# Hybrid decoder block: own-block mask applied once per head on GpSimd, score sums negated

## The chip, the core and the metric

The kernel runs on one NeuronCore of one Trainium2 chip. The metric is device time in microseconds (us) of one execution; lower is better. Engines are named as in the profile: PE (TensorE matmul), PEld (TensorE weight load), DVE (VectorE), ACT (ScalarE), POOL (GpSimd) and SP (SyncE, which only issues DMAs). Each engine works through its own instruction queue in order.

## The reference, cut to the attention branch

One decoder layer, 512 tokens, width 1024. A gated DeltaNet branch (8 heads) and a forgetting-attention branch (8 heads of 128) run on one input projection, are merged by sigmoid gates, and a squared-ReLU MLP of width 4096 follows. The change touches the forgetting attention alone:

```python
def forgetting_attention(q, k, v, log_f):
    cum = jnp.cumsum(log_f, axis=-1)
    scale = FOX_DH ** -0.5
    for i in range(t // FOX_BLOCK):          # 4 blocks of 128 queries
        q0, q1 = i * FOX_BLOCK, (i + 1) * FOX_BLOCK
        s = (jnp.einsum('bhqd,bhkd->bhqk', q[:, :, q0:q1], k[:, :, :q1]) * scale
             + cum[:, :, q0:q1, None] - cum[:, :, None, :q1])
        mask = (q0 + jnp.arange(FOX_BLOCK))[:, None] >= jnp.arange(q1)[None, :]
        p = jax.nn.softmax(jnp.where(mask, s, -jnp.inf), axis=-1)
        outs.append(jnp.einsum('bhqk,bhkd->bhqd', p, v[:, :, :q1]))
```

## The kernel before, in words

Weights stream through the core once. Each unit of weights (128x1024 float32) is loaded into a raw tile, rounded by ACT into `hi` (L243, in the MLP L1366) and subtracted by DVE into `lo` (L244, L1373), so that PE can multiply in three passes. In the second half of the input projection (`stream`, L988, tiles `st`) and in the MLP the weights are combined in a Strassen-like scheme: some raw tiles are first loaded by SP (L204) and later changed in place by an accumulating DMA that POOL issues (L208, `sraw`).

The branches run as generators (`fox_worker`, `head`, `group_chain`, `decays`, ...) that `tick()` advances between pieces of the projection. What comes out is a program order; a scheduler of the framework then fixes the order on each engine's queue from its own estimate of when inputs are ready. A change of one instruction can therefore move others.

`fox_worker` handles one attention head at a time (two workers from the middle of the kernel on). For a head it takes `nr`, a 128x512 tile `row` in which every partition holds the negated forget sums of the head's 512 keys; SP loads it (L530, `row<-rowd`, one of three `row` buffers). Then: squares of q and k (ACT L859, DVE L860, L861), a power on POOL (L335, `fss`), scaling of q and k on POOL (L865), transposes on PE, copies to `qT`, `kT` on ACT (L878, L879). Then for each of the four query blocks i, with n = 128(i+1) keys:

- the bias tile (two buffers): ACT adds the query's own sum to the first n-128 columns (L892, not for i = 0), and DVE writes the last 128 columns as row + sum + causal mask (L893, `scalar_tensor_tensor`, from the SBUF tiles `nr` and `caus`);
- PE multiplies q and k (L896, `sc`), DVE adds the bias and takes the row maximum in one instruction (L899, shown as CUSTOM_DVE), DVE negates the maximum (L901, a 128x1 `tensor_scalar`), ACT takes the exponential with that shift and sums it (L902);
- one step later DVE inverts the sum and scales (L908, L909), PE transposes (L912, `pT`), ACT copies out (L914), and a step later PE multiplies by v (L921, `fo`).

At the same time the second DeltaNet group runs: `head` (L588, L590, L606, L630, L639, L641 on POOL) and `invert` (L655 to L687, `X`, `tmp`).

Of the kernel before, what the change touches and what calls it, by code (L numbers as in the profile page):

```python
# [6 lines left out]
                             make_lower_triangular, make_upper_triangular)  # L7

F32 = mybir.dt.float32
F32R = mybir.dt.float32r  # L10
AF = mybir.ActivationFunctionType
ALU = mybir.AluOpType
# [4 lines left out]
P = 128  # L17
# [4 lines left out]
NCH = T // P  # L22
# [22 lines left out]
def hybrid_block(tc, a, out):  # L45
    nc = tc.nc
# [20 lines left out]
    def nm(s):  # L67
        n_names[0] += 1
        return f"{s}_{n_names[0]}"
# [5 lines left out]
    def page(dt=F32, s="pg"):  # L75
        if s in FOX_TAGS:
            return fxp.tile([P, T], dt, tag=s, name=nm(s))
        tag = TAGS_OF.get(s, s)
        if tag in TAGS:
            return pgp.tile([P, T], dt, tag=tag, name=nm(s), bufs=TAGS[tag])  # L80
        return pgp.tile([P, T], dt, tag="pg", name=nm(s))
# [3 lines left out]
    def const(shape, s, dt=F32):  # L85
        return (cp if s in KEEP else cm).tile(shape, dt, tag=s, name=s)

    def small(n, s="sm"):
        return smp.tile([P, n], F32, tag="sm", name=nm(s))
# [12 lines left out]
    def atps(s="at"):  # L102
        return pat.tile([P, T], F32, tag="at", name=nm(s))

    def v3(ap, n):
        return ap.rearrange("p (a b) -> p a b", a=n)

    def bc(ap, n):
        return ap.unsqueeze(2).to_broadcast(list(ap.shape) + [n])

    def cs(c):
        return slice(c * P, (c + 1) * P)

    mm = nc.tensor.matmul
    vec, act, pool = nc.vector, nc.scalar, nc.gpsimd
# [23 lines left out]
    def start(gen):  # L139
        tasks.append(gen)  # L140
        return gen
# [3 lines left out]
    def store_late(dst, src):  # L145

        for _ in range(LATE):
            yield
        nc.sync.dma_start(dst, src)
# [169 lines left out]

    upper = const([P, P], "upper")  # L320
    make_upper_triangular(nc, upper, diag=True)
    caus = const([P, P], "caus")
    make_causal_mask(nc, caus, mask_val=-1e30)
    slow_ = const([P, P], "slow_")
    make_lower_triangular(nc, slow_, diag=False)
    slow = const([P, P], "slow", F32R)
# [7 lines left out]
    def rsq(dst, src):  # L334
        pool.tensor_tensor(dst, src, expo[:, 0:src.shape[-1]], op=ALU.pow)  # L335
# [115 lines left out]
    cc = const([P, NCH, H], "cc")  # L451
# [387 lines left out]
    def bias_rows(n):  # L839

        if n < len(fq) and n not in rows_of:
            rows_of[n] = row_page(2, fq[n][0])
        return rows_of.get(n)

    def fox_worker(after=None):

        while after is not None and not inverted[after]:
            yield
        while taken[0] < H:
            if taken[0] >= len(fq) or hold[0]:  # L850
                yield
                continue
            h, qk, vt = fq[taken[0]]
            nr = bias_rows(taken[0])
            taken[0] += 1
            sq = small(16, "fss")
            for half in range(2):
                junk = page(s="junk")
                act.activation(junk, qk[half], AF.Square)  # L859
                vec.tensor_reduce(sq[:, 4 * half:4 * half + 4], v3(junk[:, :], 4), axis=AX.X, op=ALU.add)  # L860
            vec.tensor_scalar(sq[:, 0:8], sq[:, 0:8], 1.0 / P, EPS, op0=ALU.mult, op1=ALU.add)  # L861
            rsq(sq[:, 8:16], sq[:, 0:8])
            for half in range(2):
                t = v3(qk[half][:, :], 4)
                pool.tensor_tensor(t, t, bc(sq[:, 8 + 4 * half:12 + 4 * half], P), op=ALU.mult)  # L865
            yield
            yield
            bias_rows(taken[0])
            ptq = atps("fqT")
            ptk = atps("fkT")  # L870
            for tb in range(NCH):
                t = qk[tb // 2]
                i = tb % 2
                nc.tensor.transpose(ptq[:, cs(tb)], t[:, cs(2 * i)], ident)
                nc.tensor.transpose(ptk[:, cs(tb)], t[:, cs(2 * i + 1)], ident)
            qT = page(s="fq")
            kT = page(s="fk")
            act.activation(qT, ptq, AF.Copy, scale=fqs)  # L878
            act.activation(kT, ptk, AF.Copy, scale=fk_g)  # L879
            yield  # L880
            while not vt:
                yield
            po = None
            st = {}
            for step in range(NCH + 2):
                i = step
                if i < NCH:
                    n = (i + 1) * P
                    s = cs(i)
                    bias = page(s="bias")  # L890
                    if i:
                        act.activation(bias[:, :n - P], nr[:, :n - P], AF.Identity, bias=cc[:, i, h:h + 1])  # L892
                    vec.scalar_tensor_tensor(bias[:, s], nr[:, s], cc[:, i, h:h + 1], caus,  # L893
                                             op0=ALU.add, op1=ALU.add)
                    psc = atps("sc")
                    mm(psc[:, :n], qT[:, s], kT[:, :n], start=True, stop=True)  # L896
                    sm = small(4, "fsm")
                    pt = page(s="p")
                    vec.tensor_tensor_reduce(out=pt[:, :n], in0=psc[:, :n], in1=bias[:, :n], scale=1.0,  # L899
                                             scalar=-3.0e38, op0=ALU.add, op1=ALU.max, accum_out=sm[:, 0:1])  # L900
                    vec.tensor_scalar(sm[:, 1:2], sm[:, 0:1], -1.0, None, op0=ALU.mult)  # L901
                    act.activation(pt[:, :n], pt[:, :n], AF.Exp, bias=sm[:, 1:2], accum_out=sm[:, 2:3])  # L902
                    st[i] = [pt, sm]
                i = step - 1
                if 0 <= i < NCH:
                    n = (i + 1) * P
                    pt, sm = st[i]
                    vec.reciprocal(sm[:, 3:4], sm[:, 2:3])  # L908
                    vec.tensor_scalar(pt[:, :n], pt[:, :n], sm[:, 3:4], None, op0=ALU.mult)  # L909
                    pT = atps("pT")  # L910
                    for c in range(i + 1):
                        nc.tensor.transpose(pT[:, cs(c)], pt[:, cs(c)], ident)  # L912
                    pTs = page(s="pTs")
                    act.copy(pTs[:, :n], pT[:, :n])  # L914
                    st[i] = pTs
                i = step - 2
                if 0 <= i < NCH:
                    if po is None:
                        po = atps("fo")
                    for c in range(i + 1):  # L920
                        mm(po[:, cs(i)], vt[c], st[i][:, cs(c)], start=(c == 0), stop=(c == i))  # L921
                yield
            o = page(s="ob")
            act.copy(o, po)
            stores.append(start(store_late(obd[h], o)))
# [139 lines left out]
    box = {}  # L1065
    start(decays(0, box, gt))
    fws = [start(fox_worker())]
    ch0 = gdn_group(0, box)
    fox_pair(0)
# [7 lines left out]
    hold[0] = False  # L1077
    finish(fu)
    fws += [start(fox_worker()) for _ in range(1, NFW)]


# [272 lines left out]
    for k, (w, c, p, s_) in enumerate(MLP):  # L1354
# [6 lines left out]
        n = pos[0]  # L1361
# [121 lines left out]
```

## Time and profile before

| | before |
|---|---|
| median of 3 runs | 999.35 us (997.99 to 1000.86) |
| profiled execution | 998.66 us, of which the span is 997.0 us |
| PE busy | 979.5 us (98%) |
| DVE busy | 721.9 us (72%) |
| ACT busy | 595.7 us (60%) |
| POOL busy | 233.1 us (23%) |
| granted TensorE clock | 1.00 over the span |

The span runs from the first to the last instruction; 1.66 us of the profiled execution lie around it. An idle time stands in square brackets behind an instruction, with what ended it: `[0.56 <-DVE p L909]` means that the engine stood idle for 0.56 us until L909 was done. An engine that shows no bracket was busy until then.

### The profile page before, as it was taken

The numbers are of one execution on the slowest core, as the hardware profiler recorded it, in microseconds if no ns is written. First come the engines' busy times: TensorE is split into PE (matmuls) and PEld (weight loads), VectorE is DVE, ScalarE is ACT, GpSimd is POOL, SyncE is SP. The second block draws the span as 40 slices with busy tenths as digits, with TensorE's granted clock in tenths as the row PEclk, the third lists the DMA queues.
The fourth block names the chain that finished last, engine by engine and source line by source line (L and its number), as shares of the span: only waits on it lengthen the run. The fifth ranks groups of instructions, "written<-read, shape, count | busy, mean of one in ns | idle before, by whom it ended". The sixth has DMA issues, their size and how long they took to land.

```text
span 997.0 us, 17216 instructions
## 1 busy us (share of the span) xinstructions
PE 979.5 (98%) x6545; PEld 880.3 (88%) x6545; DVE 721.9 (72%) x1268; ACT 595.7 (60%) x1018; POOL 233.1 (23%) x230
## 2 busy tenths in 40 slices
PE   8999999999999989999999999999999999999997
PEld 6788899998888979999998888789989989988985
DVE  6878768657576789856655635779896697697695
ACT  7766454656564576766755512578855765666661
POOL 1444120102532512312230004412021121121110
PEclk9999999999999999999999999999999999999999
DMA  7647552475437866656887735587898888889845
GB/s 261 224 125 217 171 154 86 132 243 176 134 118 203 176 146 167 159 138 170 227 198 198 277 105 171 118 194 157 205 168 201 188 174 203 183 175 196 193 83 140
DMA packets 93155, 173.34 MB, mean 174 GB/s; under 512 B 7984, under 2 KB 49168, under 8 KB 93072
## 3 DMA queue, kind: packets, MB, share of 16 engines
q1 hardware_dynamic: 78640, 119.81, 37.8%
q0 software_dynamic: 14432, 52.44, 30.0%
q8 instruction: 51, 0.84, 0.3%
q14 instruction: 32, 0.26, 0.1%
HBM read 151.20 MB, written 21.02 MB: 173 GB/s over the span
## 4 chain that ended last, share of the span: by engine, by line
PE 77%; DMA 8%; DVE 6%; issue 6%; ACT 2%; POOL 1%; SPq 0%; POOLq 0%; ACTq 0%; DVEq 0%
PE mlp L1148 30%; PE st L988 9%; PE mm L266 6%; PE mm L263 6%; PE mm L262 6%; PE fx L941 2%; PE fx L939 2%; PE fx L938 2%; DMA sraw<-w_st 2%; DMA draw<-w_d 2%; DMA row<-rowd 2%; PE fo L921 2%; PE sc L896 2%; DVE lo L244 1%; DVE conv L588 1%
## 5 line engine op out<-in xcount | busy, mean ns | idle before, releaser
L1366 ACT CAST hi<-draw 128x1024 fp32r<-128x1024 f32 x124 | 129.8, 1050 | 126.2 <-PE mlp L1148 98.2
L1373 DVE TENSOR_TENSOR lo<-draw,hi 128x1024 fp32r<-128x1024 f32 x124 | 151.5, 1223 | 51.8 <-ACT hi L1366 48.9
L1148 PE MATMUL mlp<-hi,shi 128*128 128x512 f32 x280 | 109.7, 392 | 2.5 <-ACT hi L1366 1.5
L1148 PE MATMUL mlp<-lo,shi 128*128 128x512 f32 x280 | 109.1, 390 | 0.5 <-DVE lo L1373 0.5
L1148 PE MATMUL mlp<-hi,slo 128*128 128x512 f32 x280 | 109.1, 390 | 0.0
L243 ACT CAST hi<-raw 128x1024 fp32r<-128x1024 f32 (+1 forms) x62 | 62.8, 1022 | 74.9 <-PE mm L263 52.3
L244 DVE TENSOR_TENSOR lo<-raw,hi 128x1024 fp32r<-128x1024 f32 (+1 forms) x62 | 74.2, 1202 | 25.4 <-ACT hi L243 12.0
L1148 PE MATMUL mlp<-slo,hi 128*128 128x256 f32 x448 | 90.3, 283 | 0.0
L1148 PE MATMUL mlp<-shi,lo 128*128 128x256 f32 x448 | 90.3, 283 | 0.0
L1148 PE MATMUL mlp<-shi,hi 128*128 128x256 f32 x448 | 90.3, 283 | 0.0
L263 PE MATMUL mm<-ulo,hi 128*128 128x512 f32 x216 | 85.0, 394 | 1.2 <-DVE ulo L277 1.2
L262 PE MATMUL mm<-uhi,hi 128*128 128x512 f32 x216 | 85.6, 398 | 0.0
L243 ACT CAST hi<-sraw 128x1024 fp32r<-128x1024 f32 x49 | 51.2, 1046 | 34.3 <-PE st L988 18.0
L1148 PEld LDWEIGHTS mlp<-shi,hi 128*128 128x128 f32 x448 | 70.6, 192 | 0.9
L244 DVE TENSOR_TENSOR lo<-sraw,hi 128x1024 fp32r<-128x1024 f32 x49 | 60.0, 1227 | 15.2 <-ACT hi L243 12.7
L1148 PEld LDWEIGHTS mlp<-shi,lo 128*128 128x128 f32 x448 | 69.9, 192 | 0.0
L1148 PEld LDWEIGHTS mlp<-slo,hi 128*128 128x128 f32 x448 | 69.8, 192 | 0.0
L1148 PEld LDWEIGHTS mlp<-hi,shi 128*128 128x128 f32 x280 | 52.6, 188 | 14.4 <-ACT hi L1366 2.0
L1148 PEld LDWEIGHTS mlp<-lo,shi 128*128 128x128 f32 x280 | 52.6, 188 | 12.0 <-DVE lo L1373 1.0
L1148 PEld LDWEIGHTS mlp<-hi,slo 128*128 128x128 f32 x280 | 52.6, 188 | 10.3
L208 POOL DMA_DIRECT2D draw<-w_d x32 | 27.8, 869 | 141.8 <-DVE lo L1373 139.5
L266 PE MATMUL mm<-uhi,lo 128*128 128x512 f32 x216 | 57.9, 401 | 0.0
(337 smaller groups left out, 2437.5 us busy)
## 6 DMA issues: line engine op xcount, KB each, us to landing
draw<-w_u POOLq DMA_DIRECT2D x32, 512.0 KB, 5.7
draw<-w_d POOLq DMA_DIRECT2D x32, 512.0 KB, 5.8
sraw<-w_st POOLq DMA_DIRECT2D x28, 512.0 KB, 6.3
raw<-w_gdn SPq DMA_DIRECT2D x24, 512.0 KB, 3.9
draw<-w_u SPq DMA_DIRECT2D x24, 512.0 KB, 4.4
draw<-w_d SPq DMA_DIRECT2D x24, 512.0 KB, 4.4
sraw<-w_st SPq DMA_DIRECT2D x21, 512.0 KB, 5.2
hd<-hd SPq DMA_DIRECT2D x34, 256.0 KB, 4.9
```

Source lines behind the costliest of these rows:

```text
L208: nc.gpsimd.dma_start(raw, a[w][c, q, s_], accum_op=ALU.add)
L243: act.copy(hi[:, c], raw[:, c])
L244: vec.tensor_tensor(lo[:, c], raw[:, c], hi[:, c].bitcast(F32), op=ALU.subtract)
L262: mm(o, w, rhi(k), start=(k == 0), stop=False)
L263: mm(o, w, rlo(k), start=False, stop=False)
L266: mm(o, lo[:, k * cols:(k + 1) * cols], rhi(k), start=False, stop=(k == KT - 1))
L896: mm(psc[:, :n], qT[:, s], kT[:, :n], start=True, stop=True)
L921: mm(po[:, cs(i)], vt[c], st[i][:, cs(c)], start=(c == 0), stop=(c == i))
L988: mm(o, u, w, start=first and t == 0 and k == 0 and j == 0 and x is hi, stop=x is lo and k == 3, skip_group_check=True)
L1148: return (lambda *args, **kw: tc.keep_in_program_order(f(*args, **kw))) if self.pinned[0] else f
L1366: pact.copy(hi, raws[m][0])
L1373: pvec.tensor_tensor(lo, raws[m][0], hi[:, :].bitcast(F32), op=ALU.subtract)
```

## The change

Once per head, right after `nr` is taken, POOL's `affine_select` writes a copy `nd` of the row (a 128x512 page) in which each of the four 128x128 blocks is replaced by -1e30 where key > query. The last 128 columns of a bias tile are then written by ACT from `nd` (one more L892-like `activation`) instead of by DVE. The score instruction multiplies by -1 and takes the minimum instead of the maximum, so that its accumulated value is already the shift; the exponential reads with scale -1, and the negation falls. The constant `caus` and the two POOL instructions that made it fall too.

```diff
-    caus = const([P, P], "caus")
-    make_causal_mask(nc, caus, mask_val=-1e30)
...
             nr = bias_rows(taken[0])
             taken[0] += 1
+            nd = page(s="nd")
+            pool.affine_select(out=v3(nd[:, :], NCH), in_=v3(nr[:, :], NCH), compare_op=ALU.is_ge, fill=-1e30, base=0,
+                               pattern=[[0, NCH], [-1, P]], channel_multiplier=1)
...
-                    vec.scalar_tensor_tensor(bias[:, s], nr[:, s], cc[:, i, h:h + 1], caus,
-                                             op0=ALU.add, op1=ALU.add)
+                    act.activation(bias[:, s], nd[:, s], AF.Identity, bias=cc[:, i, h:h + 1])
...
-                    vec.tensor_tensor_reduce(out=pt[:, :n], in0=psc[:, :n], in1=bias[:, :n], scale=1.0,
-                                             scalar=-3.0e38, op0=ALU.add, op1=ALU.max, accum_out=sm[:, 0:1])
-                    vec.tensor_scalar(sm[:, 1:2], sm[:, 0:1], -1.0, None, op0=ALU.mult)
-                    act.activation(pt[:, :n], pt[:, :n], AF.Exp, bias=sm[:, 1:2], accum_out=sm[:, 2:3])
+                    vec.tensor_tensor_reduce(out=pt[:, :n], in0=psc[:, :n], in1=bias[:, :n], scale=-1.0,
+                                             scalar=3.0e38, op0=ALU.add, op1=ALU.min, accum_out=sm[:, 0:1])
+                    act.activation(pt[:, :n], pt[:, :n], AF.Exp, bias=sm[:, 0:1], scale=-1.0,
+                                   accum_out=sm[:, 1:2])
```

## Rows read from the trace of the kernel before

**Rows 1.** The page, first part: busy us (share of the span) xinstructions.

```profile
PE 979.5 (98%) x6545; PEld 880.3 (88%) x6545; DVE 721.9 (72%) x1268; ACT 595.7 (60%) x1018; POOL 233.1 (23%) x230
```

**Rows 2.** Stretches: us, then busy us (instructions) per engine, clock, DMA share, GB/s.

```profile
330.00:390.00 60.00, 54.58 (x429) 51.15 (x428) 51.16 (x135) 40.59 (x87) 17.85 (x17) 1.00 0.79 175
390.00:500.00 110.00, 110.00 (x1042) 105.78 (x1041) 78.42 (x206) 76.50 (x146) 27.34 (x26) 1.00 0.68 171
```

**Rows 3.** Waits of PE from 330 to 390 us: total us, times, longest.

```profile
PE pT L912 <- DVE p L909: 1.9, 3, 1.0
PE st L988 <- ACT fqk L968: 1.2, 1, 1.2
PE sc L896 <- ACT fk L879: 0.8, 1, 0.8
PE pT L912 <- DVE fsm L901: 0.7, 1, 0.7
PE ktm L120 <- ACT conv L590: 0.7, 1, 0.7
```

**Rows 4.** Groups of DVE and ACT, 100 to 500 us: xcount | busy us, mean ns | idle before.

```profile
L893 DVE SCALAR_TENSOR_TENSOR bias<-row,cc,caus 128x128 f32<-128x128 f32 x32 | 12.2, 380 | 9.7 <-DMA row<-rowd 9.7
L901 DVE TENSOR_SCALAR fsm<-fsm 128x1 f32<-128x1 f32 x32 | 4.8, 149 | 0.4
L899 DVE CUSTOM_DVE_ANT_0 p<-sc,bias 128x512 f32<-128x512 f32 x8 | 5.5, 688 | 1.4 <-PE sc L896 1.4
L892 ACT ACTIVATE bias<-row,cc 128x128 f32<-128x128 f32 x8 | 3.2, 402 | 14.0 <-DVE fsm L899 6.4 <-DMA row<-rowd 5.7 <-issue 1.5
```

**Rows 5.** DVE in order of time at 319 us: start us, us, what, [idle before].

```profile
319.31 0.35 DVE L893 SCALAR_TENSOR_TENSOR bias<-row,cc,caus 128x128 f32<-128x128 f32 x1 [5.77 <-DMA row<-rowd]
319.57 1.22 DVE L244 TENSOR_TENSOR lo<-sraw,hi 128x1024 fp32r<-128x1024 f32 x1
```

**Rows 6.** All engines in order of time, 355 to 358 us.

```profile
355.49 1.63 POOL L641 TENSOR_TENSOR conv<-conv,row 128x512 f32<-128x512 f32 x1
...
355.74 0.14 DVE L901 TENSOR_SCALAR fsm<-fsm 128x1 f32<-128x1 f32 x1
355.79 1.49 DVE L893 SCALAR_TENSOR_TENSOR bias<-row,cc,caus 128x128 f32<-128x128 f32 x1
...
357.20 0.27 DVE L909 TENSOR_SCALAR p<-p,fsm 128x128 f32<-128x128 f32 x1
...
357.53 0.33 PE L912 MATMUL pT<-ident,p 128*128 128x128 f32 x1 [0.56 <-DVE p L909]
```

**Rows 7.** DVE in order of time, 360 to 364 us.

```profile
360.90 2.07 DVE L658 STREAM_TRANSPOSE E<-dg 128x1024 f32<-128x1024 f32 x1
362.88 0.32 DVE L909 TENSOR_SCALAR p<-p,fsm 128x256 f32<-128x256 f32 x1
```

**Rows 8.** All engines in order of time, 383 to 386 us.

```profile
383.18 2.09 POOL L865 TENSOR_TENSOR fqk<-fqk,fss 128x512 f32<-128x512 f32 x2
...
384.29 1.26 DVE L909 TENSOR_SCALAR p<-p,fsm 128x512 f32<-128x512 f32 x1
...
385.70 0.63 PE L912 MATMUL pT<-ident,p 128*128 128x128 f32 x4 [0.36 <-DVE p L909]
```

**Rows 9.** ACT, and after the dots PE, in order of time, 343 to 353 us.

```profile
346.02 1.05 ACT L243 CAST hi<-sraw 128x1024 fp32r<-128x1024 f32 x1 [5.00 <-DMA sraw<-w_st]
348.57 0.40 ACT L892 ACTIVATE bias<-row,cc 128x128 f32<-128x128 f32 x1 [1.50 <-DVE fsm L899]
...
350.17 0.92 PE L896 MATMUL sc<-fk,fq 128*128 128x128 f32 x4 [0.85 <-ACT fk L879]
```

**Rows 10.** Groups of POOL over the whole span, the one existing select.

```profile
masks.py:30 POOL TENSOR_SCALAR_AFFINE_SELECT caus<-caus 128x128 f32<-128x128 f32 x1 | 0.3, 302 | 0.0
```

**Rows 11.** POOL in order of time, behind the row's landing at 319.3 us.

```profile
320.96 1.03 POOL L335 TENSOR_TENSOR ssk<-ssk,expo 128x4 f32<-128x4 f32 x1 [8.39 <-DVE ssk L606]
```

**Rows 12.** Loads of `row` tiles, 100 to 480 us: time to landing.

```profile
DMA to landing us min/median/max: 2.6/6.8/8.5
```

More of the change, by code (lines that the diff above doesn't have):

```diff
@@ L5 @@
 from concourse import mybir
-from concourse.masks import (make_causal_mask, make_identity,
-                             make_lower_triangular, make_upper_triangular)
+from concourse.masks import (make_identity, make_lower_triangular, make_upper_triangular)
 F32 = mybir.dt.float32
@@ L907, in fox_worker @@
                     pt, sm = st[i]
-                    vec.reciprocal(sm[:, 3:4], sm[:, 2:3])
-                    vec.tensor_scalar(pt[:, :n], pt[:, :n], sm[:, 3:4], None, op0=ALU.mult)
+                    vec.reciprocal(sm[:, 2:3], sm[:, 1:2])
+                    vec.tensor_scalar(pt[:, :n], pt[:, :n], sm[:, 2:3], None, op0=ALU.mult)
                     pT = atps("pT")
```

## The prediction

> **What bounds the kernel now.** I read the page's busy shares first: PE is busy for 979.5 of 997.0 us [rows 1], so all the time that PE ever stands idle is 17.5 us, and no edit off PE can gain more. The change leaves PE's instructions as they are. Next I cut the span into stretches and looked where PE is idle while the attention heads run. From 390 to 500 us PE is busy for all 110 us; from 330 to 390 us it is busy for 54.58 of 60 us [rows 2]. So 5.42 us are to be had there, and the rest of the 17.5 us lies outside the attention (start, the change-over to the MLP, the tail). In this stretch DVE is busy for 51.16 us and ACT for 40.59 [rows 2]: DVE is the engine that feeds PE late. The waits of PE name what ends its idle time: scaled probabilities, copies, transposed heads [rows 3]. Only after this did I look at the cost of the edited lines; a saving on an engine is worth what it takes out of these five rows.
>
> **What the change takes off DVE.** Each of 32 blocks loses L893, on average 0.380 us, and L901, 0.149 us [rows 4]: 17.0 us by durations. Instructions on DVE overlap at their ends, so the queue moves on by less: 0.26 us from the start of an L893 to the next instruction (319.31 to 319.57) [rows 5], and 0.05 us from an L901 to the next (355.74 to 355.79) [rows 6]. That is 0.31 us a block, 9.9 us in all. Eight of the blocks lie between 330 and 390 us: 2.5 us by starts, 4.2 us by durations.
>
> **What it puts on ACT.** 32 activations of 128x128 from SBUF. The same form and line exists 8 times: 0.402 us [rows 4], so up to 12.9 us in all and 3.2 us for eight blocks. ACT has 19.4 us idle in the 60 us [rows 2], which hides them as long as they don't stand in front of something that PE waits for; without that cover the 3.2 us are the price. An own-block of i = 0 is new on ACT's queue, and it can stall there: the eight L892 of this form stood idle 6.4 us for a bias buffer that DVE's score instruction still read [rows 4], and what is queued behind it (`hi` copies, `qT`, `kT`) stalls too. The score instruction, on DVE, now always waits for ACT.
>
> **What it puts on POOL.** Eight selects of 128x512. The trace has one of 128x128: 0.302 us [rows 10]; the nearest 128x512 are two two-input multiplies that took 2.09 us together, 1.05 each [rows 8]. The ends are thus 0.30 and 1.05 us. I take 0.7, the middle, since the shape is that of the one and the operation that of the other: 5.6 us in all on an engine with 42 of 60 us idle [rows 2]. The select waits for the row's DMA, and POOL's queue behind it holds powers for both branches, scalings, and the accumulating DMAs of the weight stream.
>
> **What stays.** The score instruction keeps operands and shape; only the sign and the reduction differ. Its own row is the nearest: 0.688 us for 128x512 [rows 4]. I take no difference; were it to run twice as long, the widest block would cost DVE 0.69 us more, were the changed form leaner, a like amount less is the other end, and no row excludes either. The exponential with a scale, no added table load, and the two POOL instructions of `caus` at the start: nothing, PE doesn't wait for them.
>
> **The sum, from PE's idle rows.**
> 1. At 319.31 DVE executes an L893 for which it stood idle 5.77 us, since the row's DMA had not landed [rows 5]; a `lo` conversion of weights was queued right behind. POOL was idle at that time (8.39 us until the power at 320.96 [rows 11]), so the select can wait there instead, and DVE can go on. With the select of 0.7 us after the landing at 319.3, POOL's power comes at 320.0 and is no later than 320.96. PE's 0.7 us wait for `ktm`, which needs a convolution that DVE makes in this backlog [rows 3], goes: -0.7.
> 2. At 355.79 an L893 takes 1.49 us instead of 0.34, beside a POOL multiply of 1.63 us from 355.49; L909 and PE's transposes follow, and PE stood idle 0.56 us [rows 6]. L893 is gone: -0.56.
> 3. At 362.88 the scaling L909 comes behind a DVE transpose of 2.07 us [rows 7]; PE waits 0.7 us, put down to L901 [rows 3]. By then three blocks have been through the stretch, 3 x 0.31 = 0.93 us of DVE time, so a DVE without gaps is ahead by more than the wait: -0.7.
> 4. At 384.29 L909 takes 1.26 us beside POOL's scaling of a head, PE waits 0.36 us, and 1.2 us for `fqk` shortly after [rows 3, 8]. DVE will be ahead here, but whether it misses POOL's instruction is chance: I take half of 1.56, -0.78.
> 5. The `sc` wait of 0.85 us and the longest wait for `p`, 1.0, stand behind a weight tile that landed late; ACT idled 5.00 us for it, then 1.50 for a bias buffer [rows 3, 9]. The select adds to the queue that issues such loads, and the bias buffer is still waited for: I take 0, with 1.9 as the bound.
>
> Together -2.7 us. Against the profiled execution, 998.66 us (span 997.0 and 1.66 around it), that makes 995.96; the median of the runs is 0.69 above that execution, so **996.7** on its scale. The bounds of the terms are 0 and -5.4 (all idle time of the stretch): 994.0 to 999.4.
>
> **A rule on the port.** An L893 took 1.49 us instead of 0.34 beside a POOL instruction [rows 6]. The Trainium skill, "SBUF — State Buffer", Who interferes with whom, says that a DVE instruction with two SBUF inputs contends with a GpSimd instruction that reads SBUF, and that whichever is issued second is blocked until the first ends. By that rule, with which the row agrees, eight selects that read SBUF are eight new chances to block DVE's `lo` conversions, and 32 two-input instructions that could be blocked are gone. If each select held one conversion up for its whole 0.7 us, 5.6 of the 9.9 us saved on DVE would go back, and scaled by what is left the sum would be -1.2 us; by the rows alone it stays at -2.7.
>
> **Rivals.**
> - *All of it goes.* DVE's lead also brings the loads of step 5 forward, since an accumulating DMA waits for DVE's `lo` before it. For: the backlog begins with the 5.77 us at 319 [rows 5]. Against: ACT's added work. -4 to -5.4 us: about 994.5.
> - *Nothing moves.* The stalls pass from DVE to ACT: in the same eight blocks ACT takes on up to 3.2 us, and each select blocks a DVE instruction by up to 1.49 - 0.34 = 1.15 us [rows 6], 9.2 us for eight, nearly the 9.9 that DVE saves. For: L892 already waits for buffers [rows 4]. Against: ACT's idle share. About 999, between 997.5 and 1000.5.
> - *Slower: POOL waits where DVE waited.* A row takes 2.6 to 8.5 us to land, 6.8 in the middle [rows 12]. A select placed on POOL's queue ahead of an accumulating DMA holds that up by as much. The price of one such lateness is in the trace: ACT idle 5.00 us, PE idle 0.85 and 1.0 us after it [rows 3, 9], 1.9 us. It decides from the point at which the select waits for over some 5 us with a weight load behind it. Bias instructions waited for a row twice on DVE [rows 4]; two such cases and no gain elsewhere give 999.35 + 3.8 = 1003.2.
> - *Slower: the score waits for ACT.* The eight own-blocks of i = 0 stall on ACT's queue as the eight L892 of this form do, 6.4 us [rows 4], and PE sees the share that it saw at 350 us, 0.85 of 1.50 [rows 9]: 3.6 us. It decides from the point at which ACT's copies for PE stand behind the wait. 1003.0.
>
> **How the numbers follow.** Two medians of this kernel can be told apart from about 0.3%, 3.0 us. The forecast (-1.5 to -4) has 0.44, and half of it lies beyond 3 us; all gone 0.18; nothing moves 0.20; POOL's queue 0.12; the score behind ACT 0.06. Faster by over 0.3%: 0.22 + 0.18 = 0.40. Within: 0.22 + 0.20 = 0.42. Slower: 0.18. The range runs from 993.0 (the best bound, 994.0, and 1 us for the scatter of medians) to 1002.0, which leaves out the centres of both slower rivals, some 0.15 with the tail below.
>
> **What would show it.** The profile after should show no L893 and L901, 17 us less DVE and some 13 us more ACT, POOL up by 2.4 to 8.4 us, and PE idle between 330 and 390 us down from 5.42 to about 2.7. Step 1 is right if DVE has no wait for `row` any more and POOL has one. Step 2 and 3 are right if the waits of `pT` for `p` shrink. The prediction is wrong if POOL's select stands ahead of a late `sraw` load, if PE's waits now name `bias` through ACT, or if the scheduler's new order makes gaps in a stretch that has none now, which no row of before can show.

## The result and the profile after

The changed kernel takes 991.87 us (median, 990.29 to 995.36) against 999.61 (996.98 to 1001.83) for the kernel before on the same chip: a ratio of 0.9933, 95% interval 0.9916 to 0.9949. The forecast was 996.7 with a range from 993.0: the direction was right, the gain of 7.7 us is 2.9 times the 2.7 that the sum gave, and it lies outside the range.

The first lines of the page of after, its stretches (columns as in [rows 2]) and every wait of PE from 100 to 560 us:

```profile
span 990.4 us, 17193 instructions
PE 978.6 (99%) x6545; PEld 881.4 (89%) x6545; DVE 711.6 (72%) x1204; ACT 603.2 (61%) x1050; POOL 239.9 (24%) x236
```

```profile
330.00:390.00 60.00, 60.00 (x489) 58.19 (x488) 52.81 (x127) 46.55 (x105) 20.84 (x20) 1.00 0.82 183
390.00:500.00 110.00, 109.80 (x1028) 105.25 (x1027) 70.21 (x170) 78.60 (x156) 35.05 (x31) 0.98 0.70 176
```

```profile
PE pT L911 <- ACT pTs L913: 0.2, 1, 0.2
```

Set beside [rows 1]: DVE has 10.3 us less, ACT 7.5 more, POOL 6.8 more. Set beside [rows 2, 3]: PE's 5.42 idle us between 330 and 390 are gone to the last hundredth, and none of the five waits of [rows 3] is left. That is the greater part of the 6.6 us by which the span shrank. PE's idle time over the whole span went from 17.5 to 11.8 us: -5.4 in this stretch, -0.9 from 500 us on, +0.4 in the first 100 us and +0.2 from 390 to 500. The other 0.9 us is busy time (979.5 to 978.6). The medians differ by 1.2 us more than the two profiled executions (998.66 and 992.12), because the one of before lay 0.95 us under the median of its six runs and the one of after 0.25 over it.

The new and changed instructions, for [rows 4, 10]. First the groups of ACT from 100 to 500 us, then the select (min/median/max in ns):

```profile
L893 ACT ACTIVATE bias<-nd,cc 128x128 f32<-128x128 f32 x32 | 12.5, 392 | 0.8 <-POOL nd L854 0.8
```

```profile
L854 POOL TENSOR_SCALAR_AFFINE_SELECT nd<-row x8: 647/874/1327, 128.7 to 448.7; 128x512 f32<-128x512 f32 x8
```

The own block costs ACT 0.392 us (0.402 was assumed). A select takes 0.874 us in the middle and 1.327 at most (0.7 was assumed, bounds 0.30 and 1.05), and POOL never stood idle for its row. ACT waited for a select twice, 0.8 us in all, and PE not at all. Neither of the two slower rivals happened.

### The profile page after: what moved, and what is told of

It is laid out like the page before. It is cut to its first block, busy times and chain, and to the rows that moved or that the text cites. A ratio compares the mean times of both kernels' runs of the same rounds, so it can differ in the third digit from the quotient of the medians.

```text
span 990.4 us, 17193 instructions
## 1 busy us (share of the span) xinstructions
PE 978.6 (99%) x6545; PEld 881.4 (89%) x6545; DVE 711.6 (72%) x1204; ACT 603.2 (61%) x1050; POOL 239.9 (24%) x236
## 4 chain that ended last, share of the span: by engine, by line
PE 89%; DMA 3%; issue 3%; DVE 2%; ACT 2%; POOL 0%; SPq 0%; POOLq 0%; ACTq 0%; DVEq 0%
PE mlp L1147 30%; PE st L987 14%; PE mm L265 8%; PE mm L261 8%; PE mm L262 8%; PE fx L940 2%; PE fx L938 2%; PE fx L937 2%; DMA draw<-w_d 2%; PE fo L920 2%; PE sc L895 2%; PE pT L911 1%; PE kk L625 1%; PE kq L633 1%; PE v L773 1%
## 5 line engine op out<-in xcount | busy, mean ns | idle before, releaser
L1147 PEld LDWEIGHTS mlp<-hi,slo 128*128 128x128 f32 x280 | 52.6, 188 | 10.3
```

Source lines behind the costliest of these rows:

```text
L1147: return (lambda *args, **kw: tc.keep_in_program_order(f(*args, **kw))) if self.pinned[0] else f
```

## The experiments

The change has a mask half (select on POOL, own block on ACT) and a sign half (negated sum, minimum, no negation). In the expectations, theory A says that DVE has less to do, theory B that DVE no longer waits for the row in front of other work, theory C that any edit reshuffles the queues and the gain is the luck of one order, and theory D that the negation no longer stands in DVE's in-order queue between the score and the exponential.

| kernel | median us | ratio to before, 95% interval | lowest run less lowest of before, us | PE busy, 330 to 390 |
|---|---|---|---|---|
| after | 991.87 | 0.9933 [0.9916, 0.9949] | -6.7 | 60.00 |
| e1 mask half alone | 999.39 | 1.0009 [0.9993, 1.0024] | +1.2 | 57.17 |
| e2 sign half alone | 994.95 | 0.9975 [0.9958, 0.9992] | -3.9 | 58.23 |
| e14 the same once more | 995.75 | 0.9968 [0.9954, 0.9981] | -4.1 | 58.24 |
| e8 negation moved to ACT | 998.92 | 0.9980 [0.9960, 1.0001] | -2.5 | 56.51 |
| e10 sign half, idle negation kept | 996.53 | 0.9952 [0.9935, 0.9969] | -2.5 | 56.07 |
| e3 after, masked row by DVE | 991.74 | 0.9938 [0.9923, 0.9954] | -6.5 | 60.00 |
| e5 after, own block by DVE | 994.06 | 0.9926 [0.9911, 0.9941] | -4.7 | 60.00 |
| e13 after, both by DVE | 990.87 | 0.9926 [0.9906, 0.9945] | -5.9 | 59.48 |
| e7 after, idle two-input work on DVE | 994.84 | 0.9970 [0.9958, 0.9983] | -3.6 | 58.48 |
| e15 after, idle one-input work on DVE | 993.07 | 0.9941 [0.9920, 0.9962] | -5.3 | 58.61 |
| e6 before, idle selects on POOL | 1004.67 | 1.0046 [1.0027, 1.0064] | +4.8 | 54.99 |
| e4 before, a fourth row buffer | 1003.67 | 1.0057 [1.0037, 1.0077] | +4.3 | 58.43 |

The median of before was 998.49 us beside e1, e2, e3 and e7, 1000.62 beside e5, e6, e8 and e10, and 998.58 beside e4, e13, e14 and e15. So ratios are compared, not microseconds. The lowest runs are added because single runs of one kernel scatter by up to 10 us (995.06 to 1004.81 in e8); how many runs stand behind each differs (4 to 12, and 6 to 25 for before), so they are a rough scale. The last column is one stretch of one execution: e4 is fuller there than before and yet slower.

### Each half alone: e1, e2, e14

e1 is the change without its sign half:

```diff
-scale=-1.0, scalar=3.0e38, op0=ALU.add, op1=ALU.min, accum_out=sm[:, 0:1])
+scale=1.0, scalar=-3.0e38, op0=ALU.add, op1=ALU.max, accum_out=sm[:, 0:1])
+vec.tensor_scalar(sm[:, 1:2], sm[:, 0:1], -1.0, None, op0=ALU.mult)
```

> Mask half of the change alone: the masked row comes from POOL, ACT writes the own block, but the maximum and its negation on DVE stay. Theory A (DVE load): DVE is late between 330 and 390 us because it has too much to do, and the gain goes with the DVE time taken away. 32 x 0.26 = 8.3 of the 9.9 us go, so most of the gain: 993 to 994 us, PE idle under 1 us between 330 and 390. Theory B (row wait): the gain comes from DVE no longer standing 5.77 us for a row at 319 us. Then all of it is here: 992 us. Theory C (order): any edit reshuffles the queues and the gain is the luck of one order; then this one may land anywhere from 992 to 1002.

e2 and e14 are the kernel before with the sign half:

```diff
-scale=1.0, scalar=-3.0e38, op0=ALU.add, op1=ALU.max, accum_out=sm[:, 0:1])
-vec.tensor_scalar(sm[:, 1:2], sm[:, 0:1], -1.0, None, op0=ALU.mult)
-act.activation(pt[:, :n], pt[:, :n], AF.Exp, bias=sm[:, 1:2], accum_out=sm[:, 2:3])
+scale=-1.0, scalar=3.0e38, op0=ALU.add, op1=ALU.min, accum_out=sm[:, 0:1])
+act.activation(pt[:, :n], pt[:, :n], AF.Exp, bias=sm[:, 0:1], scale=-1.0, accum_out=sm[:, 1:2])
```

> Sign half alone: minimum of negated sums, no negation on DVE; the own block stays on DVE with the causal constant. Theory A: 32 x 0.05 = 1.6 us (by durations 4.8) less on DVE, a gain of about 1 us: 998.5. Theory B: DVE still waits for the row, nothing moves: 999.6, and the 5.8 us wait of DVE for a row is still in the trace. Theory C: anywhere.

> The sign half alone once more, beside the three others on one chip: 0.9975 was measured (0.9958 to 0.9992), so close to no change and to the whole change (0.9933) that its share of the gain is uncertain. Theory D, with the negation's place in the chain as the main cause, gives 0.994 to 0.997; if the two halves only work together, 0.998 to 1.000.

The mask half alone is worth nothing (1.0009). The sign half alone gives 0.9975 and 0.9968, somewhat under half of the whole gain. The rest, about 0.4%, comes from the mask half, but only once the sign half is there.

In e1 no scaled probability is late for PE any more, but other things are. PE's waits from 330 to 390 us:

```profile
PE fqT L874 <- POOL fqk L865: 1.4, 1, 1.4
PE st L987 <- DVE fqk L969: 0.6, 1, 0.6
PE sc L895 <- ACT fk L879: 0.6, 1, 0.6
```

Between 100 and 330 us two more are new, 0.7 us for a convolution of DVE (`mm`) and 1.0 for one that ACT passes on (`ktm`).

So the mask half took the DVE waits for rows away (which theory B would pay for) and bought POOL's scaling of heads and late convolutions in their place.

The sign half leaves two of the five waits of [rows 3]. For e14, from 330 to 390 us:

```profile
PE pT L912 <- DVE p L909: 1.0, 1, 1.0
PE st L988 <- ACT fqk L968: 0.7, 1, 0.7
```

The first of them is step 2 of the prediction in pure form. DVE, POOL and PE of e14 in order of time:

```profile
350.89 2.46 DVE L893 SCALAR_TENSOR_TENSOR bias<-row,cc,caus 128x128 f32<-128x128 f32 x2
...
353.35 1.10 DVE L639 SCALAR_TENSOR_TENSOR am<-kq,ssk,em 128x128 f32<-128x128 f32 x4
354.37 0.41 DVE L661 COPY X<-x_id 128x512 f32<-128x512 f32 x1
354.70 0.28 DVE L909 TENSOR_SCALAR p<-p,fsm 128x128 f32<-128x128 f32 x1
```

```profile
351.32 1.62 POOL L641 TENSOR_TENSOR conv<-conv,row 128x512 f32<-128x512 f32 x1
```

```profile
355.04 0.33 PE L912 MATMUL pT<-ident,p 128*128 128x128 f32 x1 [1.03 <-DVE p L909]
```

Two L893 should take 0.7 us; they take 2.46, until just after POOL's multiply ends at 352.94, and everything behind them, the scaling L909 included, comes late: 1.03 us of PE. The mask half removes L893 from this place, and in after the wait is gone. This is the clearest part of what the mask half adds.

### Chain or load: e8, e10

e10 takes the negation out of the way of the exponential but keeps its time on DVE; e8 keeps it in the way but takes its time off DVE:

```diff
 # e10: the sign half, and
+vec.tensor_scalar(sm[:, 3:4], sm[:, 0:1], -1.0, None, op0=ALU.mult)   # read by nothing
 # e8: the kernel before, but
-vec.tensor_scalar(sm[:, 1:2], sm[:, 0:1], -1.0, None, op0=ALU.mult)
+act.mul(sm[:, 1:2], sm[:, 0:1], -1.0)
```

> Kernel before with the sign half, and DVE still executes 32 negations of 128x1, into a column that nobody reads: DVE has the same instructions as before, only the exponential no longer waits for the negation. Theory D (place in the chain): the negation cost not its 0.15 us but the DVE instructions that the queue put between it and the score instruction, up to 2.6 us for a block between 330 and 390 us; taken off the chain, the gain of the sign half stays: 994 to 996 us, against 998.5 before. Theory A (DVE load): the load is back, so the gain goes: 998 to 999. Theory C (order): anywhere from 992 to 1002.

> Kernel before, the negation moved from DVE to ACT, right ahead of the exponential on the same queue. The maximum and the exponential are as before. Theory D: the wait in DVE's queue is gone, and ACT pays some 0.2 us a block: 994 to 997. Theory A: 1.6 us less on DVE, 6 us more on ACT: 998 to 999. A part of the gain that came from the minimum or the scale of -1 itself would be missing here.

How far an exponential can stand behind its score in the kernel before is seen here, DVE and then ACT from 360 to 364 us (between the two DVE lines stand the transpose and the scaling of [rows 7]):

```profile
360.90 0.08 DVE L899 DVE_READ_ACCUMULATOR2_ANT fsm<- 128x1 f32 x1
...
363.11 0.15 DVE L901 TENSOR_SCALAR fsm<-fsm 128x1 f32<-128x1 f32 x1
```

```profile
363.29 0.51 ACT L902 ACTIVATE p<-p,fsm 128x256 f32<-128x256 f32 x1 [1.10 <-DVE fsm L901]
```

The maximum is there at 360.98. The negation that needs 0.15 us of DVE runs at 363.11, and the exponential, for which ACT stood idle 1.10 us, starts at 363.29, 2.3 us after its score. In after the same block goes like this:

```profile
356.31 0.08 DVE L898 DVE_READ_ACCUMULATOR2_ANT fsm<- 128x1 f32 x1
356.31 0.34 DVE L908 TENSOR_SCALAR p<-p,fsm 128x256 f32<-128x256 f32 x1
356.58 2.07 DVE L655 STREAM_TRANSPOSE E<-dg 128x1024 f32<-128x1024 f32 x1
```

```profile
356.85 0.51 ACT L900 ACTIVATE p<-p,fsm 128x256 f32<-128x256 f32 x1
```

0.46 us, and ACT was busy until then. Added up over all 32 blocks from such rows, the time from the end of the accumulator's read to the start of the exponential is about 57 us in before, 68 in e1 and 44 in e8, but 14 in e10, 17 in e2, 19 in after and 21 in e13 (below).

DVE's queue is only a part of this: of the 57 us in before some 22 lie between the read and the start of the negation. The rest has to do with where the exponential stands on ACT's queue. The block behind the late weight tile of [rows 9] shows it, DVE, ACT and PE of before:

```profile
348.45 0.08 DVE L899 DVE_READ_ACCUMULATOR2_ANT fsm<- 128x1 f32 x1
348.57 0.15 DVE L901 TENSOR_SCALAR fsm<-fsm 128x1 f32<-128x1 f32 x1
```

```profile
350.62 1.28 ACT L902 ACT_TABLE_LOAD   x1
351.91 0.40 ACT L902 ACTIVATE p<-p,fsm 128x128 f32<-128x128 f32 x1
```

```profile
352.63 0.29 DVE L909 TENSOR_SCALAR p<-p,fsm 128x128 f32<-128x128 f32 x1
353.07 0.30 PE L912 MATMUL pT<-ident,p 128*128 128x128 f32 x1 [1.02 <-DVE p L909]
```

Here the negation runs right behind its score, and still the exponential starts 3.4 us after the read. ACT first waits 1.50 us for a bias buffer (L892), then executes L892 and three more instructions, and only then loads its table and takes the exponential. PE's longest wait for `p` ends behind it. The same block in after:

```profile
343.89 1.28 ACT L900 ACT_TABLE_LOAD   x1
345.38 0.40 ACT L900 ACTIVATE p<-p,fsm 128x128 f32<-128x128 f32 x1 [0.20 <-DVE fsm L898]
345.78 0.39 ACT L892 ACTIVATE bias<-row,cc 128x128 f32<-128x128 f32 x1
```

The table load fills the time in which ACT would wait, the exponential follows the read within 0.04 us, and L892 comes behind it. So it is in every kernel whose exponential waits for no negation (e2, e14, e10, e3, e5, e13, e7 and e15: 0.03 or 0.04 us); in those where it does (before, e1, e4, e6, e8) this block takes 1.8 to 3.5 us. Theory C as mere luck doesn't explain such a division; that the scheduler moved the exponential because of the negation is a reading of its orders, not a test of it.

What this is worth to PE shows in e10, waits from 330 to 390 us:

```profile
PE st L989 <- ACT fqk L969: 1.2, 1, 1.2
PE pT L913 <- DVE p L910: 1.1, 1, 1.1
PE sc L896 <- ACT fk L879: 0.8, 1, 0.8
PE ktm L120 <- ACT conv L590: 0.7, 1, 0.7
PE fqT L874 <- POOL fqk L865: 0.2, 1, 0.2
```

Three of the five rows are those of [rows 3] to the tenth (1.2, 0.8, 0.7). The waits of `pT` alone fell, from 2.6 (1.9 and 0.7) to 1.1, and those 1.1 are again an L893 beside POOL's L641 (2.14 us where it takes 0.34). So in this stretch the negation off the chain is worth 1.5 us of `pT`. In e14, which has 0.15 us a block less on DVE as well, `ktm` and `sc` no longer wait; the run times don't show this second part apart. By the lowest runs e8 and e10 are each worth 2.5 us and the sign half, which does both, 4: a bit less than the sum. By medians e10 (0.9952) looks as good as the sign half and e8 (0.9980) hardly different from no change; the intervals overlap, and the shares of place and load are not settled more finely than this.

One row of [rows 3] seems to say more than it does: the 0.7 us of `pT` put down to the negation L901. The PE row behind it, of before:

```profile
363.34 0.41 PE L912 MATMUL pT<-ident,p 128*128 128x128 f32 x2 [0.71 <-DVE fsm L901]
```

What these two transposes read is the `p` that L909 scaled from 362.88 to 363.20 [rows 7]; L901 negates the maximum of another block, whose exponential only starts at 363.29. PE starts 0.14 us after the end of L909, as it does at 353.07 (0.15), where the row names L909. The negation is named because it ended last, at 363.26. PE waited for L909, and L909 for the transpose of 2.07 us in front of it. In e1, which keeps the negation, the wait is gone, and L909's counterpart stands ahead of that transpose, as in after (356.31 and 356.58 above), e10 and e14. In e4, which has before's order here, it is 0.7 again.

### Is it the work that left DVE? e3, e5, e13

```diff
 # e3 and e13: masked row by DVE, once per head
-pool.affine_select(out=v3(nd[:, :], NCH), ...)
+vec.tensor_tensor(v3(nd[:, :], NCH), v3(nr[:, :], NCH),
+                  caus[:, :].unsqueeze(1).to_broadcast([P, NCH, P]), op=ALU.add)
 # e5 and e13: own block by DVE
-act.activation(bias[:, s], nd[:, s], AF.Identity, bias=cc[:, i, h:h + 1])
+vec.tensor_scalar(bias[:, s], nd[:, s], cc[:, i, h:h + 1], None, op0=ALU.add)
```

> Whole change, but the masked row is made by DVE (row plus the causal constant, one 128x512 add per head) and not by POOL. Theory A: 8 x 0.69 = 5.5 us go back onto DVE, which leaves 4.4 of the 9.9 us: a gain of 3 to 4 us, 996. Theory B: DVE waits for the row again as before, so the gain is lost: 999 and a DVE wait for a row of several us.

> Whole change, but the own block is written by DVE from the masked row (one SBUF input) instead of by ACT. Theory A: 8.3 of the 9.9 us are back on DVE: 996 to 998. Theory D: what counts is the chain behind the score instruction, which stays short; the bias tile is ready early in any case: 991 to 994.

> The whole change, but neither POOL nor ACT takes anything over: the masked row is made by DVE once per head (eight adds, about 0.68 us each in the earlier run) and the own block is written by DVE as a one-input tensor_scalar (about 0.28 us each). If what the mask half adds to the sign half comes from the two-SBUF-input instruction that has left the blocks, the time is that of the whole change, ratio 0.992 to 0.9945. If it comes from work that left DVE, DVE now has some 14 us back and the ratio is that of the sign half alone, 0.996 to 0.999.

All three have the whole gain. e13, in which neither POOL nor ACT takes anything over, has as much DVE work as the kernel before (721.4 us against 721.9 in [rows 1]) and is as fast as after (0.9926 against 0.9933, the intervals nearly the same). The page of e13:

```profile
PE 979.8 (99%) x6545; PEld 881.7 (89%) x6545; DVE 721.4 (73%) x1244; ACT 595.4 (60%) x1018; POOL 236.2 (24%) x230
```

Theory A in its plain form, a gain through the sum of DVE's busy time, falls. That the mask goes to GpSimd isn't needed. What all three and after have in common is that the row is masked once per head, away from the blocks, and that a block is left with an instruction that reads one tile; that this and not the new order of instructions is what counts is likely and not shown. e13 doesn't beat after by anything that can be measured.

In e13 the one-input instruction is held up beside the same multiply of POOL. DVE, then POOL:

```profile
351.51 1.71 DVE L896 TENSOR_SCALAR bias<-nd,cc 128x128 f32<-128x128 f32 x1
353.14 0.28 DVE L911 TENSOR_SCALAR p<-p,fsm 128x128 f32<-128x128 f32 x1
```

```profile
351.49 1.64 POOL L641 TENSOR_TENSOR conv<-conv,row 128x512 f32<-128x512 f32 x1
```

1.71 us in place of 0.285, over 0.1 us after POOL is done. PE loses 0.41 us here and not 1.03, because the scheduler put the scaling L911 right behind, and not behind L639 and L661 as in e14:

```profile
353.47 0.33 PE L914 MATMUL pT<-ident,p 128*128 128x128 f32 x1 [0.41 <-DVE p L911]
```

So one SBUF input didn't protect the instruction beside POOL; what was queued behind the blocked one set the price.

### Work put back beside the chain: e7, e15

```diff
 # after, and per block (jd is read by nothing)
+vec.scalar_tensor_tensor(jd, bias[:, s], cc[:, i, h:h + 1], caus, op0=ALU.add, op1=ALU.add)   # e7
+vec.tensor_scalar(jd, bias[:, s], cc[:, i, h:h + 1], None, op0=ALU.add)                       # e15
+vec.tensor_scalar(sm[:, 3:4], sm[:, 0:1], -1.0, None, op0=ALU.mult)                           # both
```

> Whole change plus the DVE time that it saved: per block one 128x128 instruction like L893 that reads the bias tile, and one 128x1 negation, both into tiles that nobody reads. DVE has its old load, but no wait for the row. Theory A: the waits of PE between 330 and 390 us come back: 998 to 1000. Theory B: DVE still has no row wait: stays at 992 to 993.

> The whole change, with an unread one-input tensor_scalar of 128x128 and an unread negation added to DVE per block: the same as the run that put an unread two-input instruction there (0.997), but with one SBUF input. If the number of SBUF inputs is what costs, the ratio is that of the whole change, 0.992 to 0.9945; if any instruction at that place costs, or the DVE time does, it is near 0.997 again.

Both lose 1.4 to 1.5 us of PE time between 330 and 390 us again, both where PE can't write the projection's output `st` until ACT, in e7 DVE too, has copied queries and keys out of it (`fqk`). e7 gives 0.9970, clearly less than the whole gain, and e15 0.9941, which can't be told from it; the two intervals overlap (0.9958 to 0.9962), so that the second SBUF input is the cause is not shown. With e13, which has nearly as much DVE work and the whole gain, e7 suggests that the place of an instruction on DVE counts, and not its time alone.

### The price of the select: e6

```diff
 # the kernel before, per head (nd is read by nothing)
+nd = page(s="nd")
+pool.affine_select(out=v3(nd[:, :], NCH), in_=v3(nr[:, :], NCH), ...)
```

> Kernel before plus the eight selects on POOL, whose result nobody reads; nothing taken off DVE or off the chain. It shows what the select costs by itself, with its page, its place on POOL's queue and the new order. Theories A and D: 0 to +1 us, 998 to 1000. The rival of the prediction (POOL waits where DVE waited): +2 to +4, 1000 to 1003. Theory C: a move of several us in either direction although no engine that PE waits for has gained or lost work.

Eight selects that nothing reads make the kernel before 0.46% slower. The dearest place, POOL, DVE and PE in order of time:

```profile
384.85 0.92 POOL L208 DMA_DIRECT2D sraw<-w_st  x1 [0.23 <-DVE fsm L911]
...
384.99 4.32 DVE L912 TENSOR_SCALAR p<-p,fsm 128x512 f32<-128x512 f32 x1
...
385.49 2.35 POOL L868 TENSOR_TENSOR fqk<-fqk,fss 128x512 f32<-128x512 f32 x2
...
387.49 1.52 POOL L857 TENSOR_SCALAR_AFFINE_SELECT nd<-row 128x512 f32<-128x512 f32 x2
...
389.36 0.90 PE L915 MATMUL pT<-ident,p 128*128 128x128 f32 x3 [2.36 <-DVE p L912]
```

A scaling that takes 0.4 us lasts 4.32, until POOL's train of a DMA issue, two multiplies and two selects has ended at about 389.0, and PE stands idle for 2.36 us. The rule of the Trainium skill, "SBUF — State Buffer", Who interferes with whom, that `tensor_scalar` too can enter a two-port mode, and that it then contends with GpSimd and is blocked while GpSimd has the port, agrees with this row and with the 1.71 us of e13. Two of the selects stand in this train, so their price is real, and the prediction's fear that a select blocks DVE was right in kind. A wait of POOL for a row is not what made it. In after the longest of the 32 scalings takes 1.637 us, and PE waits for none:

```profile
L908 DVE TENSOR_SCALAR p<-p,fsm x32: 278/416/1637, 165.7 to 480.4; 128x128 f32<-128x128 f32 x8, 128x256 f32<-128x256 f32 x8, 128x384 f32<-128x384 f32 x8, 128x512 f32<-128x512 f32 x8
```

### The row alone: e4

```diff
-rwp = mix.enter_context(tc.tile_pool(name="rwp", bufs=3))
+rwp = mix.enter_context(tc.tile_pool(name="rwp", bufs=4))
```

One page of the page pool made room for it (53 to 52).

> The kernel before with a fourth row buffer (one page fewer in the page pool), so that a row is loaded earlier and DVE has less to wait for at 319 us; nothing else is changed. If the 5.77 us for which DVE stood behind a row were worth what step 1 put on them, 0.7 us are gained (ratio 0.9993) and, if they begin the whole backlog of 330 to 390 us, up to 5.4 (0.9946). Theory D (the negation's place in the chain) gives no change, ratio 0.999 to 1.001.

It became 0.57% slower. With a buffer free earlier, the scheduler placed the own-block instruction one round of convolutions earlier on DVE's queue, and the row wasn't there. DVE, PE and stretches of e4:

```profile
294.63 2.31 DVE L588 SCALAR_TENSOR_TENSOR conv<-mm,c_conv,conv 128x511 f32<-128x511 f32 x3
308.61 0.35 DVE L893 SCALAR_TENSOR_TENSOR bias<-row,cc,caus 128x128 f32<-128x128 f32 x1 [11.67 <-DMA row<-rowd]
```

```profile
316.28 0.77 PE L262 MATMUL mm<-uhi,hi 128*128 128x512 f32 x1 [5.60 <-DVE conv L588]
```

```profile
310.00:316.00 6.00, 0.68 (x3) 0.21 (x2) 4.84 (x11) 0.00 (x0) 2.24 (x2) 0.96 0.52 148
316.00:320.00 4.00, 3.72 (x9) 3.01 (x10) 3.96 (x9) 1.57 (x2) 0.00 (x0) 0.50 0.56 169
```

The stretch of before that has DVE's wait of 5.77 us for the row, at 319 [rows 5]:

```profile
300.00:330.00 30.00, 30.00 (x163) 25.53 (x162) 22.39 (x47) 12.16 (x30) 11.09 (x10) 1.00 0.68 178
```

That wait left PE busy for all of the 30 us; one of 11.67 costs 5.6 us. So the row on DVE was slack that was nearly used up, not a loss. This fits with e14, which keeps a wait of 5.25 us for the row at 317.81 and has the gain of the sign half, and with e1, which has no such wait and no gain. Theory B falls as the cause by itself.

## Why the prediction was wrong

The steps of the sum are the five waits of [rows 3], and all five went.

- **Step 1 (-0.7, `ktm`).** The effect came, the cause is not the one named: e10 and e14 both keep DVE's wait for the row (5.22 and 5.25 us), and only e14 is rid of the `ktm` wait. What showed it was to be a wait of POOL for the row; POOL had none.
- **Step 2 (-0.56).** Right in mechanism. e14 isolates it at 1.03 us: L893 beside POOL's multiply, and L909 late behind both.
- **Step 3 (-0.7).** Right in size and in the row that it went by, L909 behind the transpose of 2.07 us. Its reason, a DVE that is 0.93 us ahead, is not what the rows show: in after the scaling stands ahead of that transpose. The order on DVE's queue changed, which the sum could not know. e7 and e15 have the old order there without the wait, so the new order isn't the only way out of it.
- **Step 4 (-0.78, half of 1.56).** All of it went in after. The `fqk` part of it, 1.2, is the one that comes back first: e7, e10 and e15 all have it or a wait like it.
- **Step 5 (0, with 1.9 as the bound).** This is the step that failed: it was put at nothing, because the bias buffer would still be waited for, and 1.85 us went. In after ACT doesn't wait for that buffer here: the table load and the exponential stand ahead of L892, and in place of the 1.50 us there are 0.20 for the score. e10 is rid of the 1.0 us for `p` in this way, although its weight tile is nearly as late as before (4.89 us). Behind it stands the cost of L901. The prediction gave it 0.05 us of DVE's queue in each of 32 blocks and nothing for the exponential that waits for it, but without the negation in between, the exponential came forward in each kernel.

The `sc` half of step 5 has another part. ACT's wait for the weight tile, 5.00 us in [rows 9], is 1.79 in after:

```profile
342.82 1.05 ACT L242 CAST hi<-sraw 128x1024 fp32r<-128x1024 f32 x1 [1.79 <-DMA sraw<-w_st]
```

It is 3.75 in e14 and 1.84 in e1: both halves shorten it, the mask half more. The loads came forward, as the rival "all of it goes" had said (at 0.18); that rival has the right size, though not by DVE's load alone. With step 4 whole and step 5 at its bound the sum would have been -5.4.

The remaining 1.2 to 2.4 us lie where the prediction saw nothing to win: its bound of -5.4 took one stretch's idle time as all there is. From 500 us on PE idles 0.9 us less, and its busy time shrank by 0.9 us, so idle time alone was no bound. Why busy time shrank was not followed up.

The costs were about right: select 0.874 us, own block 0.392 us, the score instruction as before (0.689 us for 128x512 against 0.688 in [rows 4]), POOL +6.8 us (2.4 to 8.4 forecast), ACT +7.5 (some 13 were named as what would show; the 32 new instructions take 12.5), DVE -10.3 (by starts 9.9 was worked out, and 17 by durations wrongly named as what would show). Of the two slower rivals neither mechanism was seen: POOL's selects didn't wait for a row, and the 12.6 us for which DVE waited ahead of score instructions were all for PE. e6 (+4.8 us by the lowest runs) shows that selects can cost as much in another way, by a DVE instruction blocked beside POOL, which the prediction's paragraph on the port had in mind for the `lo` conversions.

What stays open: how the sign half divides between place and load; why e2 and e14, with 1.7 us of waits left in this stretch, are 2.6 to 2.8 us behind after by the lowest runs and some 4 us by ratios of medians; and how much of each difference is the scheduler's new order. No run here holds the order fixed. A part of the scatter is the granted clock: of e2's ten runs the two with a mean clock of 1.000 took 992.2 and 992.4 us, the eight with 0.995 to 0.998 took 994.5 to 1001.1. It doesn't settle the question, for at a like clock of 0.998 after took 991.6 and 992.1, and e2 995.05.

## What to carry to other kernels

Cost a tiny instruction by its place and not by its duration: measure from the end of what it needs to the start of what needs it, over all its occurrences, and look where its reader stands on the reader's own queue and what could run there meanwhile, a table load above all. Before you build on a wait that names an instruction, check that the waiting instruction reads its result: the row names what ended last. And where the change frees the engine that feeds the bound one, take "all listed waits go" as a main case, since the waits of one stretch tend to hang together.

## What the runs showed of the chip

- A one-input `tensor_scalar` of DVE was held up by POOL like a two-input instruction: 4.32 us for 0.4 (e6), 1.71 for 0.285 (e13).
- The granted clock fell to 0.50, its 1.2 GHz level, for 316 to 320 us in e4, after PE had been busy for 0.68 of 6 us. In after it fell too, with PE busy throughout, right behind some 95 matmuls of 32x32 from 428 to 431 us:

```profile
430.00:435.00 5.00, 5.00 (x58) 4.96 (x53) 1.20 (x4) 2.07 (x6) 0.00 (x0) 0.66 0.28 104
```

The kernel before executes the same matmuls at 1.00 throughout in its profiled execution [rows 2], so neither they nor a busy PE decided it. In e5 and e15 the clock fell at 433 and 432 us as well.
